# Seven block products for eight in the first feed-forward step's way down, with raw weights asked for two chunks ahead

## The chip, the cores and the metric

One core of one Trainium2 chip. The metric is the device time of one execution in microseconds (us). The engines are TensorE (PE: matmuls, PEld: its weight loads), VectorE (DVE), ScalarE (ACT), GpSimd (POOL) and SyncE (SP); SP and POOL also issue the transfers (DMA), each from a queue of its own that runs in order.

## The reference

One layer of a hybrid decoder over 576 rows (512 of a prompt, 8 x 8 of samples), 1024 channels wide, all in float32:

```python
x = x + 0.5 * swiglu(rmsnorm(x, ffn1_norm), w_gate, w_up, w_down)   # 2816 hidden channels
x = x + concat(y_lru, y_pool) @ w_out                               # mixer, from rmsnorm(x) @ w_in
x = x + cross_attend(rmsnorm(x, xattn_norm), mem_k, mem_v, wq, wo)  # 4 heads, 256 memory rows
x = x + 0.5 * swiglu(rmsnorm(x, ffn2_norm), w_gate, w_up, w_down)
y = rmsnorm(x, final_norm)

def swiglu(x, w_gate, w_up, w_down):
    return (silu(x @ w_gate) * (x @ w_up)) @ w_down
```

The change lies in the two feed-forward steps, called f1 and f2 here, which share one function.

## The kernel before, in words

Activations stand with channels on the 128 partitions and the 576 rows along the free side, so x is eight panels of 128 x 576. Each float32 operand is split into a high and a low part (`split`, L175 to L182: ACT rounds the high part, DVE subtracts it), and each product is three matmuls of high x high, high x low and low x high; a matmul has 128 x 128 weights and 288 columns, half of the rows.

**The way up.** The 2816 hidden channels are 22 chunks of 128. The first three of f1 and the first two of f2 are computed plainly (`std`). Every other chunk takes gate and up together as one 2 x 2 block product with seven block products for eight (Strassen's form, as Winograd wrote it), named by their weights: 11, E, F, G, 12, H and 22, twelve matmuls each. E, F, G and H are sums of the raw blocks 11, 12, 21 and 22. One pass of the loop over f (from L848) runs the products in the order 11, E, then 22 of the chunk before (`finish_chunk`), F, G, 12, H. `fill()` puts steps of the way down between them.

**The way down.** In f2, chunks 0 to 15 are taken in four groups of four (`quick`), again with seven products for eight: a column is a pair of output panels of one group, seven products of six matmuls in six steps, and there are 4 x 4 = 16 columns. Their weights come as `td` and `t2` tiles, split by `ensure`. The operands of such a group are sums of hidden chunks (`build_a`, `build_b`, into tiles `ph` and `pl`). The results go to SBUF on ACT (`take`, L659) and are added into x by an accumulating transfer on POOL's queue (L676, L703, L710). Chunks 16 to 21 go plainly (`down`, groups of two and four). In f1 all 22 chunks go plainly in five groups (`FGS`): each hidden chunk is split into `hh` and `hl`, 48 matmuls a chunk go into `pd`, and DVE adds the result into x (L554). The last group of each step runs alone after the loop; in f1 each panel of x is then squared and split for the mixer (`nm.add`).

**Where the block sums come from.** In f1 `prepare_a` and `prepare_b` load the four raw blocks (L440) and DVE makes four sums a chunk (L454 to L456, L467). In f2 two of them, for E and H, and two sums of the down weights, were made in memory earlier: `background` (L157) issues accumulating transfers on POOL's queue during f1 and the mixer into `gsum` and `dsum`. DVE makes the other two (L491, L492).

**What sets the order.** All matmuls of f1 and f2 keep their written order (`chain` in `mm`). The other engines' instructions, the transfers on SP among them, are put in order by a planner that takes what is ready by its own costs; on the chip each engine's queue then runs in that order and waits where something isn't there. Buffers limit how far ahead it goes: four tiles `wr` for raw weights (`WRB`, 4 KB a partition each), five each for the split parts `wh` and `wl` (`WSB`); one `td`. The same three tags hold all weight panels of the mixer and the attention, and there the caches too. At the start of f1 the two first panels and the squares of x by rows (`xs`, L756, five tiles in `wh` and `wl`, for the norm factor) use them.

Of the kernel before, what the change touches and what calls it, by code (L numbers as in the profile page):

```python
# [22 lines left out]
FGS = (4, 4, 4, 5, 5)  # L23
# [7 lines left out]
WRB, WSB = 4, 5  # L31
# [38 lines left out]
def hybrid_step(ctx, tc, a):  # L70
# [45 lines left out]
    neg = const.tile([P, 4 * DC], F32, name="neg")  # L116
    v.tensor_scalar(neg, cst[:, :4 * DC], -1.0, None, op0=ALU.mult)

    def ncol(name, i=0):
        c = _C[name] + i  # L120
        return neg[:, c:c + 1]


    s.activation(const.tile([P, 1], F32, name="table"), ones, AF.Silu)
# [22 lines left out]
    nfast = FFC - STD[1]  # L147
# [3 lines left out]
    for i in range(nfast):  # L151
        w = a["f2_gu"][i].rearrange("p b k n -> p b (k n)")
        jobs.append((gsum[i], w[:, 0:2, :], w[:, 3:4, :].to_broadcast([P, 2, KP * P])))
        if i < FAST * NQ:
            w = a["f2_d"][i // NQ, i % NQ].rearrange("p b k n -> p b (k n)")
            jobs.append((dsum[i // NQ][i % NQ], w[:, 0:2, :], w[:, 3:4, :].to_broadcast([P, 2, 2 * P])))
# [216 lines left out]
    def ffn(name, n, fp, turn, plain, head=False, fast=False):  # L373
# [3 lines left out]
        wstd, wgu, wd = a[f"{name}_s"], a[f"{name}_gu"], a[f"{name}_d" + "p" * fast]  # L377
# [7 lines left out]
        def small_tile(nm_):  # L385
            return fp.tile([P, HT], F32, tag="pc", bufs=2 if fast else 3, name=nm_)

        def full_tile(nm_):
            return fp.tile([P, T], F32, tag="e", bufs=3 if fast else 2, name=nm_)
# [30 lines left out]
        def std_out(i, pg, pu):  # L420
            e = full_tile("e")
            for (p, q), (_, rr) in zip(pieces(pg, e), pieces(pg, r)):
                v.tensor_mul(q, p, rr)
            s.activation(e, e, AF.Silu, scale=-1.0)
            v.tensor_mul(e, e, half)
            for p, q in pieces(pu, e):
                v.scalar_tensor_tensor(out=q, in0=p, scalar=-1.0, in1=q, op0=ALU.mult, op1=ALU.mult)
            if fast:
                raw[i] = e
            else:  # L430
                split(hh[0][:, i, :], hl[0][:, i, :], e)
# [3 lines left out]

        def load(f):
            if f < FFC:
                raws[f] = [raw_tile(f"r{i}") for i in range(2)]
                for i in range(2):
                    nc.sync.dma_start(raws[f][i], wgu[f - plain, :, 2 * i:2 * i + 2])  # L440
# [6 lines left out]
        def prepare_a(f):  # L447
            if f >= FFC:
                return
            r0, r1 = raws[f]  # L450
            (w22, w11), (w12, w21) = ([t[:, i] for i in range(2)] for t in (r0, r1))
            w = W[f] = {}
            w["22"], w["11"] = parts_of(r0, "a")
            v.tensor_add(w22, w22, w21)  # L454
            v.tensor_add(w21, w21, w11)
            v.tensor_add(w11, w11, w22)  # L456
            w["E"], w["F"] = parts_of(r0, "e")

        def prepare_b(f):
            if f >= FFC:  # L460
                return
            r0, r1 = raws.pop(f)
            w = W[f]
            one = [fp.tile([P, KP, P], F32R, tag=tag, name=f"{tag}_b") for tag in ("oh", "ol")]
            split(*one, r1[:, 0])
            w["12"] = lambda q, k: one[q][:, k, :]
            v.tensor_add(r1[:, 0], r1[:, 0], r0[:, 1])  # L467
            w["G"], w["H"] = parts_of(r1, "g")


        def load_pairs(f):
            if f < FFC:
                w, e = wgu[f - plain], gsum[f - plain].rearrange("p b (k n) -> p b k n", n=P)
                raws[f] = [raw_tile(f"r{i}") for i in range(2)]
                for (i, b), src in zip(((0, 0), (0, 1), (1, 0), (1, 1)), (e[:, 0], w[:, 1], w[:, 2], e[:, 1])):
                    nc.sync.dma_start(raws[f][i][:, b], src)

        def load_22(f):
            if f < FFC:
                raw22[f] = wp.tile([P, KP, P], F32, tag="wr", bufs=WRB, name="r22")  # L480
                nc.sync.dma_start(raw22[f], wgu[f - plain, :, 0])

        def prepare_e(f):
            if f < FFC:
                W[f] = {}
                W[f]["E"], W[f]["11"] = parts_of(raws[f][0], "e")

        def sum_g(f):
            if f < FFC:
                r0, r1 = raws[f]  # L490
                v.tensor_add(r0[:, 1], r0[:, 1], r0[:, 0])  # L491
                v.tensor_add(r0[:, 0], r0[:, 1], r1[:, 0])  # L492

        def prepare_g(f):
            if f < FFC:
                W[f]["G"], W[f]["F"] = parts_of(raws[f][0], "g")
# [12 lines left out]
        groups = PLAIN if fast else [(sum(FGS[:i]), FGS[i]) for i in range(len(FGS))]  # L509
        panels = [(gi, j) for gi in range(len(groups)) for j in range(DC)]  # L510
        fetched, wdown = {}, {}

        def fetch(i):

            if i < len(panels) and i not in fetched:
                gi, j = panels[i]
                c0, fg = groups[gi]
                c0 -= PLAIN[0][0] * fast
# [3 lines left out]
        def make(i, pool=None):  # L522

            if i < len(panels) and i not in wdown:
                fetch(i)
                gi, j = panels[i]
                if pool is None:
                    w = [fp.tile([P, groups[gi][1], P], F32R, tag=tag, bufs=2 + fast, name=f"{tag}{j}")
                         for tag in ("dh", "dl")]
                else:  # L530
                    w = [pool.tile([P, groups[gi][1], P], F32R, name=f"t{q}{j}") for q in "hl"]
# [3 lines left out]
        def down(gi, after=None):  # L535

            c0, fg = groups[gi]
            pd = {}

            def step(j, k):  # L540
# [8 lines left out]
                if k == fg - 1 and fast:  # L549
# [3 lines left out]
                elif k == fg - 1:  # L553
                    v.tensor_add(halves(x[:, j, :]), pd[j][:, :, :HT], halves(x[:, j, :]))  # L554
                    if after:
                        after(j)
# [9 lines left out]
        hh, hl = {}, {}  # L566

        def group(gi):
            for d, tag in ((hh, "hh"), (hl, "hl")):
                d[gi] = fp.tile([P, FGS[gi], T], F32R, tag=tag, bufs=2, name=f"{tag}{gi}")  # L570

        def hidden(f):

            if fast:
                b = 2 * (f % 2)
                return [q[:, b:b + 2, :].rearrange("p h n -> p (h n)") for q in pairs[f // 2]]
            gi = max(i for i in range(len(groups)) if groups[i][0] <= f)
            return [q[gi][:, f - groups[gi][0], :] for q in (hh, hl)]
# [36 lines left out]
        def fetch_main(i):  # L615

            if i < FAST * NQ:
                g, q = divmod(i, NQ)
                t = draw[i] = fp.tile([P, 4, 2, P], F32, tag="td", name=f"td{i}")
                nc.sync.dma_start(t[:, 0:4:3], dsum[g][q].rearrange("p b (k n) -> p b k n", n=P))  # L620
                nc.sync.dma_start(t[:, 1:3], a["f2_d"][g, q, :, 1:3])

        def fetch_22(i):
            if i < FAST * NQ:
                t = draw[i, 0] = fp.tile([P, 2, P], F32, tag="t2", name=f"t2{i}")
                nc.sync.dma_start(t, a["f2_d"][i // NQ, i % NQ, :, 0])

        def ensure(n):

            while made[0] < min(n, 4 * FAST * NQ):  # L630
# [3 lines left out]
                if k == 3:  # L634
                    split(*(q[:, 0] for q in w), draw.pop((i, 0)))
                    fetch_22(i + 1)
                else:
                    if k:
                        v.tensor_add(t[:, k], t[:, k], t[:, k - 1])
                    split(*w, t[:, k:k + 2])  # L640
                    if k == 2:
                        fetch_main(i + 1)
# [72 lines left out]
        if fast:  # L715
            ts = [fp.tile([P, 2, 3, HT], F32, tag=tag, bufs=3, name=f"t_{tag}") for tag in ("ph", "pl")]
        else:
            group(0)
            ts = [fp.tile([P, 2, 3, HT], F32, tag=tag, bufs=2, name=f"t_{tag}") for tag in ("hh", "hl")]
# [3 lines left out]
        if head:  # L723
# [7 lines left out]
            for k in range(DC):  # L731
                n.split(k)
                if k % 2 == 0:
                    for raw, hi, lo in ws:
                        split(hi[:, k:k + 2, :], lo[:, k:k + 2, :], raw[:, k:k + 2, :])
# [5 lines left out]
        w = panel(wstd[1, 0], DC, P, "s")  # L741
        std(cols(ps1[0]), w, range(4))
# [20 lines left out]
        else:  # L763
            q = row_factor([n.acc], n.name, free[2], parts=3)
            for i in range(2):
# [4 lines left out]
        std(cols(ps1[1]), w, range(4))  # L770
# [7 lines left out]
        if fast:  # L778
            half = r
        else:  # L780
            half = fp.tile([P, T], F32, name=f"half_{n.name}")
            s.activation(half, r, AF.Copy, scale=0.5)
        std(cols(ps1[1]), w, range(4, DC))
        std_out(0, *ps0)
        if fast:
            load_pairs(plain)
            load_22(plain)
            prepare_e(plain)
            sum_g(plain)
            std_out(1, *ps1)  # L790
            prepare_g(plain)
            load_pairs(plain + 1)
            fetch_main(0)
            fetch_22(0)
        else:
            load(plain)
        if fast:
            pass
        elif plain > 2:
            ps2 = accumulators(2)  # L800
            std(cols(ps2[0]), panel(wstd[2, 0], DC, P, "s"), range(DC))
            std_out(1, *ps1)
            if head:
                n.sums(3, ts[1][:, 1])
            std(cols(ps2[1]), panel(wstd[2, 1], DC, P, "s"), range(DC))
# [816 lines left out]
```

## Time and profile before

| what | us |
|---|---|
| median of 3 runs (lowest to highest) | 1138.15 (1137.78 to 1138.83) |
| the profiled execution: its time, its span | 1138.62, 1136.7 |
| f1, start to the mixer's first product | 0 to 401.9 |
| of it the loop's first product, the last group of the way down | 50.7, 367.6 |
| mixer and attention | 401.9 to 742 |
| f2: first product, last group of the way down | 742, 1097.8 |
| PE, DVE, ACT, POOL busy in the span | 1118.5, 832.0, 610.9, 134.4 |
| granted TensorE clock | 0.996 |

A group's line gives code line, engine, operation, output and inputs, shape and count, then busy time in us and the mean ns of one, then the engine's idle time before it and what ended it. Matmuls overlap, so the mean of one (295 ns) is longer than the distance between two. A line of the chain of waits is start, length and what ran; a line of waits is who waited, for whom, us in total, times, longest.

### The profile page before, as it was taken

The numbers are of one execution on the slowest core, as the hardware profiler recorded it, in microseconds if no ns is written. First come the engines' busy times: TensorE is split into PE (matmuls) and PEld (weight loads), VectorE is DVE, ScalarE is ACT, GpSimd is POOL, SyncE is SP. The second block draws the span as 40 slices with busy tenths as digits, with TensorE's granted clock in tenths as the row PEclk, the third lists the DMA queues.
The fourth block names the chain that finished last, engine by engine and source line by source line (L and its number), as shares of the span: only waits on it lengthen the run. The fifth ranks groups of instructions, "written<-read, shape, count | busy, mean of one in ns | idle before, by whom it ended". The sixth has DMA issues, their size and how long they took to land.

```text
span 1136.7 us, 21329 instructions
## 1 busy us (share of the span) xinstructions
PE 1118.5 (98%) x8536; PEld 1101.0 (97%) x8536; DVE 832.0 (73%) x1387; ACT 610.9 (54%) x1052; POOL 134.4 (12%) x176
## 2 busy tenths in 40 slices
PE   8999999999999999999999999999999999999996
PEld 8999999999999999999999889999999999999996
DVE  8877778777775687986833566769878888787654
ACT  7644344344342454885622455546666666666554
POOL 0011111111111033310000000000121111212110
PEclk9999999999999999999999999999999999999998
DMA  8356766577674388642566762223675766766652
GB/s 293 117 146 152 185 167 149 140 162 188 155 182 107 103 236 191 119 141 94 174 217 215 261 229 92 66 89 93 162 176 148 182 172 160 188 167 154 148 115 84
DMA packets 82547, 179.58 MB, mean 158 GB/s; under 512 B 8272, under 2 KB 28752, under 8 KB 82320
## 3 DMA queue, kind: packets, MB, share of 16 engines
q1 hardware_dynamic: 55456, 129.66, 35.3%
q0 software_dynamic: 24064, 45.88, 22.9%
q10 hardware_dynamic: 2928, 2.67, 0.7%
q8 instruction: 67, 1.10, 0.4%
q14 instruction: 32, 0.26, 0.1%
HBM read 156.86 MB, written 34.17 MB: 168 GB/s over the span
## 4 chain that ended last, share of the span: by engine, by line
PE 91%; DVE 4%; ACT 2%; DMA 2%; issue 1%; DVEq 0%; SPq 0%; ACTq 0%
PE pu L136 23%; PE pd L136 15%; PE pc L136 11%; PE d L136 7%; PE pa L136 5%; PE q L136 5%; PE wo L136 5%; PE xo L136 5%; PE pg L136 3%; PE k L136 2%; PE v L1347 2%; PE in_l L136 2%; PE in_p L136 2%; PE o L136 1%; PE s L136 1%
## 5 line engine op out<-in xcount | busy, mean ns | idle before, releaser
L136 PE MATMUL pd<-hh,dl 128*128 128x288 f32 x352 | 75.3, 295 | 0.0
L136 PE MATMUL pd<-hh,dh 128*128 128x288 f32 x352 | 75.0, 294 | 0.0
L136 PE MATMUL pd<-hl,dh 128*128 128x288 f32 x352 | 75.0, 294 | 0.0
L178 ACT CAST wh_e<-r 128x1024 fp32r<-128x1024 f32 x39 | 41.0, 1051 | 57.1 <-DVE r L456 27.5
L136 PE MATMUL d<-ph,dh 128*128 128x288 f32 x224 | 66.8, 298 | 0.2 <-ACT add_e L659 0.2
L136 PE MATMUL d<-ph,dl 128*128 128x288 f32 x224 | 66.3, 296 | 0.0
L136 PE MATMUL d<-pl,dh 128*128 128x288 f32 x224 | 66.0, 295 | 0.0
L676 POOL DMA_DIRECT2D x<-add_e x16 | 19.3, 1204 | 380.9 <-ACT dh L178 348.6
L136 PEld LDWEIGHTS pd<-hh,dh 128*128 128x128 f32 x352 | 56.3, 188 | 0.0
L136 PEld LDWEIGHTS pd<-hh,dl 128*128 128x128 f32 x352 | 56.2, 188 | 0.0
L136 PEld LDWEIGHTS pd<-hl,dh 128*128 128x128 f32 x352 | 56.1, 188 | 0.0
L179 DVE TENSOR_TENSOR wl_e<-r,wh_e 128x1024 fp32r<-128x1024 f32 x39 | 47.7, 1222 | 11.1 <-ACT wh_e L178 11.1
L178 ACT CAST wh_g<-r 128x1024 fp32r<-128x1024 f32 x39 | 41.0, 1052 | 20.2 <-DVE r L467 14.4
L179 DVE TENSOR_TENSOR wl_g<-r,wh_g 128x1024 fp32r<-128x1024 f32 x39 | 47.7, 1222 | 5.2 <-ACT wh_g L178 4.1
L178 ACT CAST dh<-wr_d 128x512 fp32r<-128x512 f32 (+2 forms) x50 | 30.9, 619 | 34.5 <-PE pd L136 14.7
L136 PE MATMUL pu<-n1l,wh_a 128*128 128x288 f32 x152 | 44.9, 295 | 0.0
L136 PE MATMUL pu<-n1h,wl_a 128*128 128x288 f32 x152 | 44.8, 295 | 0.0
L136 PE MATMUL pu<-n1h,wh_a 128*128 128x288 f32 x152 | 44.7, 294 | 0.0
L907 ACT ACTIVATE g<-g 128x576 f32<-128x576 f32 x39 | 26.8, 686 | 32.2 <-DVE g L906 32.2
L136 PEld LDWEIGHTS d<-ph,dh 128*128 128x128 f32 x224 | 42.1, 188 | 0.8 <-ACT add_e L659 0.4
L136 PEld LDWEIGHTS d<-pl,dh 128*128 128x128 f32 x224 | 42.3, 189 | 0.0
L179 DVE TENSOR_TENSOR dl<-td,dh 128x512 fp32r<-128x512 f32 x48 | 33.1, 689 | 12.5 <-ACT dh L178 9.3
(561 smaller groups left out, 4235.3 us busy)
## 6 DMA issues: line engine op xcount, KB each, us to landing
gsum<-f_gu POOLq DMA_DIRECT2D x40, 512.0 KB, 8.6
r<-f_gu SPq DMA_DIRECT2D x38, 512.0 KB, 4.1
r<-f_gu SPq DMA_DIRECT2D x60, 256.0 KB, 4.1
x<-add POOLq DMA_DIRECT2D x40, 288.0 KB, 4.4
r<-gsum SPq DMA_DIRECT2D x40, 256.0 KB, 3.9
dsum<-f_d POOLq DMA_DIRECT2D x32, 256.0 KB, 5.7
ck<-ck SPq DMA_DIRECT2D x16, 512.0 KB, 4.4
cv<-cv SPq DMA_DIRECT2D x16, 512.0 KB, 7.2
```

The source lines that it names most:

```text
L136: i = te.matmul(*args, **kw)
L178: s.copy(hi, src)
L179: v.tensor_tensor(out=lo, in0=src, in1=f(hi), op=ALU.subtract)
L676: nc.gpsimd.dma_start(x[:, j:j + 2, HT:], t, accum_op=ALU.add)
L907: s.activation(g, g, AF.Silu, scale=-1.0)
L1347: te.matmul(ps[:, m, :HD], lhsT=lhs[:, kd, ms], rhs=w[wi][:, k, :], start=kd == 0 and i == 0, stop=kd == DC - 1 and i == 2)
```

## The change

Of f1's way down, chunks 0 to 15 take the form that f2 has: `quick`, `build_a`, `build_b`, and the adds into x by transfers. The plain form of f1 goes with all its helpers (`FGS`, `group`, `hh`, `hl`, `load`, `prepare_a`, `prepare_b`, `half`); f1's last group has four chunks for five. `head` now marks f1 in the shared function: there the down weights come raw, and DVE makes two more sums a column.

In both steps the weights of the way up come raw, 11 and 21 in one tile, 12 in another, 22 in a third, all asked for two chunks ahead, for which `WRB` goes to 6 and `WSB` to 4. H = 21 + 11 and G = F + 12 are made on DVE; E = 21 + 22 and F = 11 + E are made by accumulating transfers on POOL's queue, the first from memory, the second within SBUF. So block 22 is read twice, and `gsum` with its forty transfers is gone. The sixteen jobs for f2's down weights now run beside the projections of the mixer and `w_out` alone. The inputs' blocks are stored in another order (21, 11, 12, 22).

```diff
-FGS = (4, 4, 4, 5, 5)
...
-WRB, WSB = 4, 5
+WRB, WSB = 6, 4
...
-    gsum = [scratch.tile([P, 2, KP * P], F32, name=f"gsum{i}") for i in range(nfast)]
...
-        jobs.append((gsum[i], w[:, 0:2, :], w[:, 3:4, :].to_broadcast([P, 2, KP * P])))
...
+        def load_11(f):
             if f < FFC:
+                raws[f] = [raw_tile("r0")]
+                nc.sync.dma_start(raws[f][0], wgu[f - plain, :, 0:2])
+
+        def load_12(f):
+            if f < FFC:
+                raws[f].append(raw_tile("r1"))
+                nc.sync.dma_start(raws[f][1][:, 0], wgu[f - plain, :, 2])
+
+        def sum_eh(f):
+            if f < FFC:
+                r0, r1 = raws[f]
+                v.tensor_add(r1[:, 1], r0[:, 0], r0[:, 1])
+                nc.gpsimd.dma_start(r0[:, 0], wgu[f - plain, :, 3], accum_op=ALU.add)
...
         def prepare_e(f):
             if f < FFC:
                 W[f] = {}
+                r0 = raws[f][0]
+                W[f]["E"], W[f]["11"] = parts_of(r0, "e")
+                nc.gpsimd.dma_start(r0[:, 1], r0[:, 0], accum_op=ALU.add)
+
+        def prepare_g(f):
             if f < FFC:
                 r0, r1 = raws[f]
-                v.tensor_add(r0[:, 1], r0[:, 1], r0[:, 0])
                 v.tensor_add(r0[:, 0], r0[:, 1], r1[:, 0])
+                W[f]["G"], W[f]["F"] = parts_of(r0, "g")
...
-                if k == fg - 1 and fast:
+                if k == fg - 1 and after:
+                    xj = halves(x[:, j, :])
+                    v.scalar_tensor_tensor(out=xj, in0=pd[j][:, :, :HT], scalar=0.5, in1=xj, op0=ALU.mult, op1=ALU.add)
+                    after(j)
...
+                if head:
+                    nc.sync.dma_start(t[:, 0:3], wq[g, q, :, 0:3])
+                else:
+                    nc.sync.dma_start(t[:, 0:4:3], dsum[g][q].rearrange("p b (k n) -> p b k n", n=P))
+                    nc.sync.dma_start(t[:, 1:3], wq[g, q, :, 1:3])
...
+                    elif head:
+                        v.tensor_add(t[:, 3], t[:, 0], t[:, 1])
+                        v.tensor_add(t[:, 0], t[:, 0], draw[i, 0])
...
         w = panel(wstd[1, 0], DC, P, "s")
+        load_11(plain)
+        load_12(plain)
...
+        mid = 6 if head else 4
+        std(cols(ps1[1]), w, range(mid))
```

In the loop over f the calls now stand so, between the products:

```python
product(U, w["11"], n, N11, True)      # first pass: load_11(f + 2)
product(C, w["E"], n, T1, True)        # then prepare_h(f), load_12(f + 2); first pass: sum_eh(f + 1)
finish_chunk(before)                   # then the pair operands, prepare_e(f + 1)
product(U, w["F"], n, T2, False)       # then prepare_22(f), load_22(f + 2)
product(C, w["G"], n, N22, False)      # then sum_eh(f + 2)
product(A, w["12"], n, N21, False)
product(U, w["H"], n, T3, False)       # then prepare_g(f + 1), load_11(f + 3)
```

At the start of f1 the first block sums (`sum_eh(plain)`) follow the first plain chunk, and the split for E and 11 the first half of the third; in both steps the loads for the second looped chunk and the first `td` follow ahead of the loop.

More of the change, by code (lines that the diff above doesn't have):

```diff
@@ L787, in ffn @@
             load_22(plain)
             prepare_e(plain)
-            sum_g(plain)
+            load_11(plain + 1)
+            load_12(plain + 1)
             std_out(1, *ps1)
[L791 to L805, printed above, removed]
-            prepare_a(plain)
-            std_out(2, *ps2)
-        else:
-            prepare_a(plain)
-            std_out(1, *ps1)
@@ L811, in ffn @@
[L811 to L828 removed]
+        load_22(plain + 1)
+        fetch_pair(0)
```

272 lines of the change are left out of this document (91 added, 181 removed).

## The prediction

> **What bounds the kernel now.** I read the page's totals first, then TensorE's waits, then stretches of each step, then one chunk of the second step in order of time.
>
> ```profile
> span 1136.7 us, 21329 instructions
> PE 1118.5 (98%) x8536; PEld 1101.0 (97%) x8536; DVE 832.0 (73%) x1387; ACT 610.9 (54%) x1052; POOL 134.4 (12%) x176
> PE 91%; DVE 4%; ACT 2%; DMA 2%; issue 1%; DVEq 0%; SPq 0%; ACTq 0%
> ```
>
> TensorE is busy for all but 18.2 us and carries 91% of the chain that ended last. Its waits, longest first:
>
> ```profile
> PE pg L136 <- ACT wh L178: 5.5, 1, 5.5
> PE rs L136 <- DVE rf_f L272: 1.9, 2, 1.4
> PE pg L136 <- DVE rf_n L272: 1.3, 1, 1.3
> ...
> PE d L136 <- ACT add_e L659: 0.2, 1, 0.2
> PE pd L136 <- DVE pl L179: 0.2, 1, 0.2
> ```
>
> The start (5.5), the norm factor of the first step (1.3) and the tail are the only waits of size; inside the two loops nothing over 0.2 us is left. Stretches of the first step's loop and way down, and of the second step's beginning and middle (columns: PE, PEld, DVE, ACT, POOL busy; clock; DMA share; GB/s):
>
> ```profile
> 300.00:340.00 40.00, 40.00 (x305) 40.00 (x304) 29.93 (x45) 16.38 (x25) 6.38 (x8) 1.00 0.73 179
> 367.00:402.00 35.00, 35.00 (x265) 35.00 (x264) 23.59 (x31) 17.28 (x25) 0.00 (x1) 1.00 0.41 123
> ...
> 770.00:820.00 50.00, 50.00 (x380) 50.00 (x379) 44.89 (x78) 31.94 (x60) 4.22 (x4) 1.00 0.50 129
> ...
> 860.00:900.00 40.00, 40.00 (x303) 39.87 (x302) 34.20 (x59) 27.34 (x56) 6.17 (x7) 1.00 0.66 163
> ...
> 980.00:1020.00 40.00, 40.00 (x303) 39.91 (x302) 31.85 (x55) 26.94 (x54) 7.17 (x7) 1.00 0.66 164
> ```
>
> PE is full in each, at clock 1.00. So a matmul taken away shortens the kernel by its own spacing, as long as the others keep pace. The second step already runs the seven-product way down, and its stretches show that DVE (32 to 34 of 40 us) and ACT (27) keep pace there.
>
> **The change, part by part.** First the products. The first step's way down today, the second step's, and a run of matmuls without a gap:
>
> ```profile
> L136 PE MATMUL pd<-hh,dl 128*128 128x288 f32 x352 | 75.3, 295 | 0.0
> L136 PE MATMUL pd<-hh,dh 128*128 128x288 f32 x352 | 75.0, 294 | 0.0
> L136 PE MATMUL pd<-hl,dh 128*128 128x288 f32 x352 | 75.0, 294 | 0.0
> ...
> L136 PE MATMUL d<-ph,dh 128*128 128x288 f32 x224 | 66.8, 298 | 0.2 <-ACT add_e L659 0.2
> ```
> ```profile
> 367.56 34.38 PE pd L136 x258
> ```
>
> Before: 3 x 352 = 1056 matmuls for 22 chunks, so 48 a chunk. After: 16 chunks by blocks, as the second step does, 3 x 224 = 672; six chunks plainly, 6 x 48 = 288; together 960. Removed are 96. They overlap (295 ns each), so the price is the spacing, 34.38 / 258 = 0.133 us: **96 x 0.133 = -12.8 us**. All of them stood in stretches with PE full. The rest of the step's matmuls is unchanged.
>
> Next the work beside them. In the first step DVE loses two of four weight sums a chunk, its split of each hidden chunk and most adds into x; it gains operand sums, more down splits, and two sums of `td` a column that the second step had from memory. Rather than net these I take the second step's loop, which is the same code, and add the `td` sums. The loop's period there:
>
> ```profile
> 875.00 1.59 PE pc L136 x12
> ...
> 893.27 1.59 PE pc L136 x12
> ...
> 900.50 1.58 PE pc L136 x12
> ...
> 910.83 1.59 PE pc L136 x12
> ...
> 915.60 1.59 PE pu L136 x12
> ```
> ```profile
> L639 DVE TENSOR_TENSOR td<-td 128x256 f32<-128x256 f32 x32 | 13.4, 420 | 0.3
> L491 DVE TENSOR_TENSOR r<-r 128x512 f32<-128x512 f32 x20 | 13.7, 687 | 0.1
> ```
>
> A chunk takes 910.83 - 893.27 = 17.6 us (product E to product E). By the stretches DVE has 31.85/40 to 34.20/40 of it to do, 14.0 to 15.0 us; about 3.1 us stay free. A column is six steps and a chunk runs seven, so the first step adds 7/6 x 2 x 0.42 = 1.0 us and keeps about 2.1. DVE stays behind TensorE's cover: 0. In the second step the sums for H and G are two of L491's size, as today, so DVE is unchanged there. ACT's 27 of 40 covers the new copies.
>
> The sums E and F become accumulating transfers on POOL's queue, 2 x 39. The trace has no such transfer that anyone soon waits for. The nearest are the adds into x:
>
> ```profile
> x<-add POOLq DMA_DIRECT2D x40, 288.0 KB, 4.4
> x<-add_e POOLq DMA_DIRECT2D x16, 288.0 KB, 6.4
> ```
> ```profile
> L178 ACT CAST wh_e<-r 128x1024 fp32r<-128x1024 f32 x39 | 41.0, 1051 | 57.1 <-DVE r L456 27.5
> ```
> ```profile
> 890.64 1.22 DVE L179 TENSOR_TENSOR wl_e<-r,wh_e 128x1024 fp32r<-128x1024 f32 x1
> 898.25 1.23 DVE L179 TENSOR_TENSOR wl_g<-r,wh_g 128x1024 fp32r<-128x1024 f32 x1
> ```
>
> E of the next chunk is asked for a chunk ahead, so its 4.4 to 6.4 us hide. F is the tight one: split of E, transfer, G's sum, split, product F. With four weight buffers for five, the split of the next E can start only when this chunk's E product ends, 893.27 + 1.59 = 894.9 (today it ended at 891.9). ACT and DVE then need 1.05 + 1.22 = 2.3 us: 897.2. The transfer lands at 901.6 to 903.6, G's sum of 0.69 ends at 904.3 at the latest, its split (2.3) at 906.6; G's buffer is free from 900.50 + 1.58. Product F of the next chunk starts at 915.60, so **about 9 us are left**. I take 0.5 us over both loops; the ends are 0 and a stall in every chunk (the third rival). A page of the Trainium skill, "DMA: Bandwidth & Descriptors", section on the SWDGE path, fits a POOL-issued transfer as 2.0 us plus bytes over 436 GB/s; for 256 KB that estimate is 2.6 us, where the rows above say 4.4 and 6.4. By the page F would have some 11 us left, and the sum would be 0.5 us lower; the measurement decides.
>
> The queues. POOL's runs in order, and the transfers for F stand among the adds into x, which wait for ACT; behind F's transfer waits G's sum, and behind that all of DVE. SP's loads come two chunks ahead and wait for one of six buffers; `td` stands behind them:
>
> ```profile
> 813.75 7.74 DMA td<-f_d
> ```
> ```profile
> POOL x L676 <- ACT add_e L659: 32.3, 8, 4.3
> SPq L476 <- DVE wl L179: 72.4, 9, 13.8
> DVE r L454 <- DMA r<-f_gu: 11.8, 7, 4.1
> ```
>
> SP already stands up to 13.8 us before such a load, and DVE waited seven times for raw weights (11.8 us) in the first step, with PE full; asking earlier can win only that hidden wait. 0.
>
> The **head**. The norm factor ends the 1.3 us wait:
>
> ```profile
> 21.25 7.79 DMA xs<-xs
> ```
> ```profile
> 29.06 1.06 ACT L757 ACTIVATE xs<-xs 64x1024 f32<-64x1024 f32 x1 [0.17 <-DMA xs<-xs]
> ```
> ```profile
> 33.09 1.16 PE L136 MATMUL pg<-ident,rf_n 128*128 128x128 f32 x8 [1.33 <-DVE rf_n L272]
> ```
>
> Today only the last of five `xs` tiles waits for the first panels' buffers; with four buffers three do. If they land together, two more squares stand in the chain, 2 x 1.06 = +2.1 us or a little more. Against it, two more k-steps (12 matmuls, 1.6 us) now run before the factor is wanted, and the raw weights no longer queue in between. Ends: -1.3 (the wait is gone) and +0.8; I take 0.
>
> The first chunk now has the pair operands of two pairs and the last norm sums at once, with no way-down steps to pass the time. The second step's start is like it: DVE 44.89 of 50, and PE full. Between 0 and +4 (two pairs at some 2 us more than the chunk can hold); I take +0.5, near that row. At the end of the step eight panels of 24 matmuls (3.2 us each) face x's add, split, square sum and panel split of four chunks on DVE: 23.59 us over eight panels is 2.9 us today. It just fits; the last hidden chunk's split has 18 matmuls to hide behind for 24, and where the second step has that it cost 0.2 (`pl`): +0.2. The mixer and attention get four split buffers for five and six raw ones for four; 0, between -0.5 and +0.5, since three panels of 6.4 us (48 x 0.133) still stand ahead. The block sums in memory for the second step's way down (POOL) move from the loop to the projections, where such jobs ran already: 0.
>
> The profiled execution took 1138.6 us with a span of 1136.7. 1138.6 - 12.8 + 0.5 + 0.5 + 0.2 = **1127.0**; it lay 0.5 above the median of the runs, 1138.15, so the forecast is **1126.5 us**. Its own range is 1123.5 to 1129.
>
> **Rivals.** (1) *Part is given back*, 1129 to 1135: the first chunks' DVE queue (+4), or `td` stuck behind waiting raw loads on SP. For: DVE 90% busy at 770 to 820, SP's 13.8. Against: no wait of PE over 0.2 there. At the middle of it, +5: 1131.5.
> (2) *The head gains too*: the 1.3 us go and no stall comes: 1138.15 - 12.8 - 1.3 = 1124.0, and with a half more in the middle 1123.5.
> (3) *Slower: G's sum on DVE waits for F's transfer.* DVE runs in order; if each chunk's sum is reached w us before the transfer lands, DVE loses w, has 2.1 us free in the first step and 3.1 in the second, and the rest falls on PE. From 19 x (w - 2.1) = 11.6, w = 2.7 us, the gain is gone; at w = 3.1 it costs 19 us: 1145.5. For: 4.4 against 6.4 us of landing is 2.0 us of spread, and a blocked add into x holds POOL up to 4.3. Against: 9 us of slack, in which DVE has other work ready.
> (4) *It doesn't do what it says*: the loads come no earlier, because buffers free no earlier. Then the products still go: 1126.5. Only if `td`, whose landing after 7.74 us stands in today's chain, came later by 0.8 us in each of the 16 columns would 12.8 be lost and the time stay at 1138.
>
> **How the numbers follow.** Forecast 0.58, with (4)'s first form in it; part given back 0.22; head gains 0.06; slower 0.09; no change 0.05. This measurement tells 0.2% from nothing, so faster is below 1135.9 and slower above 1140.4: faster 0.86, same 0.05, slower 0.09. 1123 to 1134 takes in the forecast, the head's gain and most of (1).
>
> **What would show it.** The first step's way down with 672 matmuls on `d` and 288 on `pd`; the mixer's first product near 389 us, for 401.9; PE with 40 of 40 us in the first step's loop; no DVE wait over 2 us on a POOL transfer; a PE wait at the norm factor between 0 and 2 us. I am wrong if DVE waits for `r` by transfer about 3 us a chunk, or PE waits on `wh_g`, `dh` or `add_e` in the loops.

## The result, and the profile after

The kernel became slower: 1245.63 us (1245.16 to 1248.56) against 1137.97 us (1135.68 to 1138.83) for the kernel before on the same chip, four runs each. The ratio is **1.0955** (95% interval 1.0932 to 1.0978). The forecast was 1126.5 us with a range up to 1134.

The page of the changed kernel begins with the span and the engines; the third line is its chain of waits by engine:

```profile
span 1243.8 us, 21744 instructions
PE 1142.7 (92%) x8440; PEld 1111.9 (89%) x8440; DVE 842.0 (68%) x1478; ACT 674.0 (54%) x1251; POOL 223.6 (18%) x270
...
PE 11%; DMA 9%; issue 5%; DVE 4%; ACT 2%; POOL 2%; DVEq 0%; POOLq 0%; ACTq 0%; SPq 0%
```

The 96 matmuls are gone (8536 to 8440). But TensorE now stands for 1243.8 - 1142.7 = 101.1 us, where it stood 18.2 us. The chain could be followed back only to 831.9 us, so its shares add up to 33%; TensorE has 11 of these 33, where it had 91 of 100 before. Its busy time rose by 24.2 us although 12.8 us of matmuls are missing, so 37 us of it are not explained by the number of matmuls. The granted clock fell from 0.996 to 0.977; an estimate from that is 1243.8 x 0.019 = 24 us. The other 13 us weren't told apart.

The waits of the changed kernel (who waited, for whom, us in total, times, longest):

```profile
DVE r L464 <- DMA r<-r: 125.1, 34, 7.2
ACT wh_g L172 <- DVE r L464: 108.9, 33, 6.2
...
PE d L135 <- ACT add L619: 28.1, 17, 2.6
PE d L135 <- ACT d L642: 25.8, 11, 4.5
PE d L135 <- ACT add_e L619: 21.9, 8, 4.5
...
PE pg L135 <- DVE rf_n L266: 0.4, 1, 0.4
```

L464 is G's sum on DVE, and `r<-r` is F's accumulating transfer within SBUF. DVE waited for it 34 times in 39 chunks, 3.7 us a time. ACT waited for DVE with G's split for 108.9 us, and in the three lines of the way down that are shown TensorE waited for ACT for 75.8 us. Before, all waits of TensorE in the loops were 0.2 us or less. The last line is the wait at the norm factor, 1.3 us before.

Stretches of the changed kernel, one of f1's loop and two of f2's (columns as before: PE, PEld, DVE, ACT, POOL busy; clock; DMA share; GB/s):

```profile
300.00:340.00 40.00, 35.39 (x258) 33.98 (x256) 28.10 (x50) 21.42 (x43) 8.28 (x9) 1.00 0.63 138
860.00:900.00 40.00, 34.83 (x258) 33.95 (x257) 26.72 (x48) 22.09 (x47) 9.46 (x10) 1.00 0.73 157
920.00:960.00 40.00, 34.27 (x228) 33.80 (x228) 26.90 (x47) 20.50 (x43) 9.43 (x10) 0.88 0.71 156
```

Where TensorE was busy for 40 of 40 us, it is for 34 to 35, in both loops alike. DVE, ACT and POOL each do less in a stretch than they could, so none of them is the bound by its amount of work. In the last stretch the same busy time holds only 228 matmuls, at clock 0.88.

One chunk of f2 shows how it hangs together. DVE in order of time (start, length, what; in brackets the wait before it):

```profile
904.97 1.23 DVE L173 TENSOR_TENSOR wl_e<-r,wh_e 128x1024 fp32r<-128x1024 f32 x1 [0.66 <-ACT wh_e L172]
906.17 0.42 DVE L173 TENSOR_TENSOR dl<-t,dh 128x256 fp32r<-128x256 f32 x1
906.62 0.46 DVE L771 TENSOR_TENSOR g<-pu,g 128x288 f32<-128x288 f32 x1
907.14 0.69 DVE L173 TENSOR_TENSOR wl<-r,wh 128x512 fp32r<-128x512 f32 x1
915.00 0.69 DVE L464 TENSOR_TENSOR r<-r,r 128x512 f32<-128x512 f32 x1 [7.16 <-DMA r<-r]
915.61 0.68 DVE L173 TENSOR_TENSOR dl<-td,dh 128x512 fp32r<-128x512 f32 x1
```

POOL in the same stretch:

```profile
907.27 1.19 POOL L636 DMA_DIRECT2D x<-add_e  x1 [3.45 <-ACT wh L172]
908.77 0.92 POOL L459 DMA_DIRECT2D r<-r  x1 [0.31 <-issue]
```

ACT, and TensorE behind it:

```profile
915.77 1.04 ACT L172 CAST wh_g<-r 128x1024 fp32r<-128x1024 f32 x1 [3.42 <-DVE r L464]
916.72 0.40 ACT L619 ACTIVATE add<-d 128x288 f32<-128x288 f32 x1
```
```profile
917.18 0.40 PE L135 MATMUL d<-ph,dh 128*128 128x288 f32 x1 [2.64 <-ACT add L619]
```

The split of E ends at 906.2. In DVE's order G's sum stands only three short instructions behind it, so DVE comes to it at 907.8. F's transfer can be issued from 906.2 on, but on POOL an add into x stands first and holds the queue until 908.46. The transfer is issued at 908.77 and lands at 914.9. DVE stands for 7.16 us, with ready work behind the sum. ACT's next instruction is the split of G, so ACT stands too. Behind it stands `add<-d`, the copy that takes a finished result of the way down out of the bank that TensorE wants next. So TensorE stops for a sum whose product is far off: product F, the first to use that split, starts at 925.96.

### The profile page after: what moved, and what is told of

It is laid out like the page before. It is cut to its first block, busy times and chain, and to the rows that moved or that the text cites. A ratio compares the mean times of both kernels' runs of the same rounds, so it can differ in the third digit from the quotient of the medians.

```text
span 1243.8 us, 21744 instructions
## 1 busy us (share of the span) xinstructions
PE 1142.7 (92%) x8440; PEld 1111.9 (89%) x8440; DVE 842.0 (68%) x1478; ACT 674.0 (54%) x1251; POOL 223.6 (18%) x270
## 5 line engine op out<-in xcount | busy, mean ns | idle before, releaser
L135 PE MATMUL d<-ph,dh 128*128 128x288 f32 x448 | 140.7, 314 | 79.8 <-ACT add L619 28.1
L135 PEld LDWEIGHTS d<-ph,dh 128*128 128x128 f32 x448 | 86.5, 193 | 91.2 <-ACT add L619 32.1
L135 PE MATMUL d<-pl,dh 128*128 128x288 f32 x448 | 134.9, 301 | 0.0
L135 PE MATMUL d<-ph,dl 128*128 128x288 f32 x448 | 134.6, 300 | 0.0
L464 DVE TENSOR_TENSOR r<-r,r 128x512 f32<-128x512 f32 x39 | 27.0, 692 | 137.5 <-DMA r<-r 125.1
L172 ACT CAST wh_g<-r 128x1024 fp32r<-128x1024 f32 x39 | 40.9, 1048 | 127.3 <-DVE r L464 108.9
L135 PEld LDWEIGHTS d<-ph,dl 128*128 128x128 f32 x448 | 87.0, 194 | 0.0
L135 PEld LDWEIGHTS d<-pl,dh 128*128 128x128 f32 x448 | 86.9, 194 | 0.0
L172 ACT CAST dh<-td 128x512 fp32r<-128x512 f32 x96 | 59.4, 618 | 32.4 <-DVE td L596 16.4
L619 ACT ACTIVATE add<-d 128x288 f32<-128x288 f32 x128 | 52.2, 408 | 5.4 <-PE d L135 4.5
L173 DVE TENSOR_TENSOR wl_h<-r,wh_h 128x1024 fp32r<-128x1024 f32 x39 | 47.5, 1217 | 3.1 <-ACT wh_h L172 3.1
L172 ACT CAST wh_e<-r 128x1024 fp32r<-128x1024 f32 x39 | 41.0, 1050 | 13.2 <-PE pc L135 12.5
L172 ACT CAST wh_h<-r 128x1024 fp32r<-128x1024 f32 x39 | 40.8, 1046 | 11.8 <-PE pu L135 9.3
```

The source lines that it names most:

```text
L135: i = te.matmul(*args, **kw)
L172: s.copy(hi, src)
L173: v.tensor_tensor(out=lo, in0=src, in1=f(hi), op=ALU.subtract)
L619: s.activation(dst, src, AF.Copy, scale=0.5 * sign)
```

## The experiments

All kernels are made from the changed one. "Theory A" in the expectations is: DVE runs in order and stands at G's sum for F's transfer. The table has every kernel; f1, the middle and f2 are split by the first products of the mixer and of f2 in the profiled execution.

| kernel | time, us | f1 | middle | f2 |
|---|---|---|---|---|
| before | 1137.97 | 401.8 | 340.1 | 394.8 |
| changed | 1245.63 | 445.2 | 341.5 | 457.1 |
| F by DVE | 1149.24 | 405.9 | 341.5 | 400.8 |
| E by DVE, F by transfer | 1216.75 | 426.3 | 341.5 | 447.1 |
| E and F by DVE | 1156.19 | 405.4 | 341.5 | 408.1 |
| G's sum late | 1192.19 | 416.7 | 341.6 | 426.9 |
| G's sum late, `td` once | 1137.09 | 396.5 | 341.6 | 397.2 |
| `td` once alone | 1218.87 | 430.5 | 341.6 | 445.0 |
| F by DVE, `td` once | 1137.31 | 394.9 | 341.6 | 399.0 |
| the same, without `td`'s head sums | 1136.31 | 395.4 | 341.6 | 397.6 |
| F by DVE, two `td`, five raw tiles | 1142.98 | 403.3 | 341.6 | 396.1 |
| the same, F by an instruction of POOL | 1155.47 | 409.8 | 341.5 | 400.7 |
| F by DVE, four raw and five split tiles | 1209.89 | 437.8 | 340.3 | 429.6 |
| G's sum late, two `td`, five raw tiles | 1195.64 | 438.1 | 341.5 | 412.7 |

### F made by DVE

```diff
-                nc.gpsimd.dma_start(r0[:, 1], r0[:, 0], accum_op=ALU.add)
...
+                v.tensor_add(r0[:, 1], r0[:, 1], r0[:, 0])
                 v.tensor_add(r0[:, 0], r0[:, 1], r1[:, 0])
```

> Change kept, but F = 11 + E is made by DVE ahead of G's sum instead of by a transfer within SBUF (39 transfers fewer on POOL, 39 sums of 0.69 us more on DVE). Theory A (DVE stands in its queue at G's sum until F's transfer has landed, 125 us in 34 waits): the waits go, f1 ends near 390 us and the time is 1126 to 1136, about 1130. Rival B (POOL's queue is the cause: E's transfers and the adds into x hold each other up): at most half comes back, about 1195. Rival C (the seven-product way down overloads DVE in f1 whatever makes the sums): f2 recovers its 60 us, f1 still ends near 445 us, time about 1185.

Measured: 1149.24 us (1147.70 to 1150.13), ratio to before 1.0097 (1.008 to 1.0114). 39 sums of 0.69 us more on DVE made the kernel 96 us faster than the changed one. Theory A's mechanism holds; rivals B and C, which stood at about 1195 and 1185, fall as the main cause. But A's own number, 1126 to 1136, was too good: 13 us or more stayed lost. TensorE's longest wait in the loops and a wait of DVE in this kernel:

```profile
PE d L135 <- ACT add_e L619: 7.6, 9, 1.2
```
```profile
DVE td L598 <- DMA td<-f_d: 19.6, 12, 3.1
```

The waits at G's sum are gone, and DVE's longest wait for a transfer is now for `td`, the way down's weights.

### E made by DVE, F by transfer; then both by DVE

```diff
-                nc.gpsimd.dma_start(r0[:, 0], wgu[f - plain, :, 3], accum_op=ALU.add)
+                v.tensor_add(r0[:, 0], r0[:, 0], raw22[f])
```

> Change kept, but E = 21 + 22 is made by DVE from the raw block 22 that is loaded anyway; F stays a transfer within SBUF. Theory A: F's transfer is the one that is waited for, so the time stays near 1240 (1225 to 1255), with DVE waiting some 3 us a chunk for it. Rival B (POOL's queue): with 39 POOL transfers gone and none between the adds into x and F's transfer, most comes back, 1150 or less. Rival C: about 1245.

> Both E and F made by DVE, no weight sum by transfer in either step; the seven-product way down, the loads two chunks ahead and the buffer counts kept. It shows the products alone. Theory A: 1127 to 1140 (DVE has four sums a chunk, 16.8 of 17.6 us in f1, so a few us may come on top). Rival B: the same. Rival C: f1 still ends near 445 us, 1185 or more.

Measured: 1216.75 us with F's transfer kept (one run), and 1156.19 us (1153.56 to 1158.97; ratio 1.0163, 1.0143 to 1.0182) with both by DVE. With E by DVE most of the wait at G's sum stays:

```profile
DVE r L464 <- DMA r<-r: 97.7, 36, 6.6
```

(In both kernels block 22 of the first looped chunk is also loaded earlier, since E's sum now reads it.) Both times lie outside what theory A expected, 1225 to 1255 and 1127 to 1140. So it is F's transfer that is waited for: taking it away gains 96 us. Taking E's away gains 29 us, and the wait for F's falls by 27 us with it. That part fits rival B (E's transfers on POOL's queue make F's later), though DVE's order changed with it. Where F's is gone, taking E's away too loses 7 us, but that isn't the price of the sums alone: DVE then stands at E's sum for the raw block 22, 31.1 us in 34 waits. E's own reader is not held up: in the changed kernel's list of waits ACT doesn't stand at E's split for a transfer. E's transfer is asked for a chunk ahead and has the time it needs, as the prediction had it.

### G's sum held back

All transfers stay. G's sum is tied to the last instruction of product H of the chunk before, which moves it back in DVE's order.

```diff
-                v.tensor_add(r0[:, 0], r0[:, 1], r1[:, 0])
+                i = v.tensor_add(r0[:, 0], r0[:, 1], r1[:, 0])
+                if f > plain:
+                    tc.add_manual_dep(i.ins, latest[0].name, ...)
```

> Change kept with all its transfers; only G's sum is bound to come after product H of the chunk before, so that it stands some 15 places behind the split of E in DVE's queue instead of 7. Nothing is taken off POOL or DVE. Theory A: the transfer then lands while DVE has other work, the wait for it falls from 3.2 us a chunk to under 0.5, time 1127 to 1140. Rival B: no change, about 1245, since POOL's queue is as before. Rival C: no change in f1, about 1185 to 1245.

Measured: 1192.19 us (1186.91 to 1195.19), ratio 1.0474 (1.0444 to 1.0504), 53 us better than the changed kernel with the same work and the same transfers, though theory A had expected 1127 to 1140. The wait at G's sum, 125.1 us before, is nearly gone, and others have come up:

```profile
DVE dl L173 <- ACT dh L172: 49.2, 28, 4.5
...
DVE td L601 <- DMA td<-f_d: 28.2, 14, 4.2
...
DVE r L464 <- DMA r<-r: 1.5, 2, 1.0
```
```profile
PE d L135 <- ACT add L622: 29.0, 26, 2.3
```

One refill of `td` in this kernel, DVE's last split of the old column and SP's loads of the next:

```profile
909.42 0.69 DVE L173 TENSOR_TENSOR dl<-td,dh 128x512 fp32r<-128x512 f32 x1
```
```profile
910.14 0.53 SPq L584 DMA_DIRECT2D td<-dsum  x1
910.72 0.66 SPq L585 DMA_DIRECT2D td<-f_d  x1
```

The load goes out 0.03 us after the split ends. SP was not late here: there is one `td` tile, it is free only when its last reader is done, and what is loaded is wanted at once. The next split of it on DVE starts at 919.0. It is the same at all 30 refills of this kernel, 15 in each step: the load (in f2 the first of two) goes out at most 0.08 us after the last split.

### `td` loaded once

The two kernels above again, with `td` loaded for the first column of each step and used for all sixteen. So 30 columns' loads are left out, and these kernels don't compute the reference's result.

```diff
-                t = draw[i] = fp.tile([P, 4, 2, P], F32, tag="td", ...)
+                if not i:
+                    t = draw[i] = fp.tile([P, 4, 2, P], F32, tag="td", ...)
...
+                if i:
+                    t = draw[i] = draw[0]
+                elif head:
                     nc.sync.dma_start(t[:, 0:3], wq[g, q, :, 0:3])
```

> F made by DVE, `td` loaded for the first column alone and used again by the other 15 (their loads are left out, all sums and splits stay). Theory A2: all of the `td` wait goes, 1125 to 1132. Rival D (DVE's work): 1143 or more.

> G's sum late as in the run before, all weight sums by transfer kept; the `td` tile is loaded for the first column alone and used again by the other 15 (their loads are left out, all sums and splits stay). Theory A2 (with G's sum late, SP stands longer at the raw load behind it and `td` comes late): 1130 to 1145 for 1192. If F's transfer still costs by itself (POOL's queue, rival B): 1175 or more.

> The changed kernel, with F's transfer as it is, but in both steps the tile td is loaded for the first of the 16 columns alone and used for all (30 td loads are left out, so the down weights of the other columns are not the reference's; the small t2 is still loaded). Theory A, DVE stands at G's sum for F's transfer: that wait stays, L464 near 125 us, and the time with it: 1205 to 1245 us. Theory T, the late td tile is the main cause and F's wait only its shadow: 1140 to 1160, with L464's wait under 30 us.

Measured, one run each: 1137.31 us with F by DVE (11.9 less than with the loads), 1137.09 with G's sum late (55.1 less), and 1218.87 where nothing else is altered (26.8 less). The last two lie where theory A2 and theory A had them; the first is 5 us above A2's 1125 to 1132. In the kernel with nothing else altered the wait at G's sum is as it was:

```profile
DVE r L464 <- DMA r<-r: 124.1, 37, 6.9
```

So `td` alone is not the cause, and theory T falls. With G's sum late and `td` out of the way, the 39 transfers for F cost next to nothing against 39 sums on DVE, and win nothing either (1137.09 and 1137.31). A distance that is enough for a sum is seen there; DVE in order of time in the kernel with the late sum and `td` once:

```profile
874.30 1.23 DVE L173 TENSOR_TENSOR wl_e<-r,wh_e 128x1024 fp32r<-128x1024 f32 x1 [0.65 <-ACT wh_e L172]
...
886.66 0.68 DVE L464 TENSOR_TENSOR r<-r,r 128x512 f32<-128x512 f32 x1
```

The sum stands 11.1 us behind the end of E's split (875.5) and waits for nothing. In the changed kernel's chunk DVE came to it after 1.6 us.

### Two `td` tiles

A second `td` tile, for which one raw tile is given up.

```diff
-WRB, WSB = 6, 4
+WRB, WSB = 5, 4
...
-                t = draw[i] = fp.tile([P, 4, 2, P], F32, tag="td", ...)
+                t = draw[i] = fp.tile([P, 4, 2, P], F32, tag="td", bufs=2, ...)
```

> F made by DVE, and two `td` tiles for one, paid for by five raw weight buffers for six. Theory A2 (what is left after F, 23 us over the forecast, is DVE standing at the sums of `td` until its load has landed, since the single tile is asked for only when the column before has been read): f1 ends near 392 us for 405.9, time 1127 to 1136. Rival D (DVE's own work, 88% of f1's loop, is too much): no better than 1149, f1 still ends past 402. Rival E (raw loads two chunks ahead are needed): slower than 1149.

> The changed kernel whole, all its transfers kept, with G's sum held back until product H of the chunk before (1192.2 with one td tile) and two td tiles, for which the raw tiles go from six to five. If the two causes found, DVE standing at G's sum and the single td tile refilled 5 us after its last reader, are all of the loss of size, DVE is spared the 27 us of sums that the kernel with F by DVE and two td tiles (1143.0) has, and the time is 1137 to 1143; below 1137 it would beat the kernel before. If instead the five raw tiles hold the loads for the transfers back (four of them cost 61 us), or the late sum makes the split of G late for its product, it is 1150 to 1190, with waits of DVE or ACT on a transfer from f_gu into r of over 1 us a chunk.

Measured with F by DVE: 1142.98 us (1140.47 to 1145.48), ratio 1.0042 (1.0029 to 1.0056). That is 6.3 less than with one `td` tile and the best time of a changed kernel that does the whole computation; it doesn't reach the kernel before. Theory A2 had expected 1127 to 1136 and an end of f1 near 392 us; f1 ends at 403.3, and DVE still waits 9.4 us for `td`. Rival D, no better than 1149, and rival E, slower than that, fall by the time, though f1 does end past 402 us, as D had it.

Measured with G's sum late and both transfers: 1195.64 us (1191.59 to 1197.23), ratio 1.0499 (1.0469 to 1.0529). This was expected at 1137 to 1143 and is no better than with one `td` and six raw tiles (1192.19). Lines of this kernel's waits, one load of `td` on SP, and DVE around it:

```profile
SPq L452 <- DMA r<-r: 108.7, 26, 8.6
```
```profile
DVE td L601 <- DMA td<-f_d: 28.2, 13, 5.5
...
ACT wh_e L172 <- DMA r<-f_gu: 19.7, 4, 6.0
```
```profile
159.45 0.92 SPq L582 DMA_DIRECT2D td<-f_d  x1
```
```profile
158.74 0.68 DVE L173 TENSOR_TENSOR dl<-td,dh 128x512 fp32r<-128x512 f32 x1
...
168.19 0.43 DVE L601 TENSOR_TENSOR td<-td 128x256 f32<-128x256 f32 x1 [4.99 <-DMA td<-f_d]
168.53 0.45 DVE L829 TENSOR_TENSOR g<-g,rstd_n 128x288 f32<-128x288 f32 x1
```

The wait for `td` is as large as with one tile (28.2 us in 13 waits, for 28.2 in 14). SP isn't late here either: the load goes out 0.03 us after the split that reads the tile last ends, at 159.42. But with two tiles DVE's first sum of a column stands a whole column earlier in its order, ahead of all three splits of the column in between, and again DVE stands at it until the load has landed, 4.99 us here, with work of the way up (L829) behind it. As with G's sum, the planner put the reader early, and the second tile bought nothing.

The five raw tiles cost as well. The raw tile that F's transfer writes is held until that has landed and the late sum and split are done. SP stands at raw loads for it for 126.6 us in all (108.7 of them in the line shown), where it stood 94.6 us with six tiles and one `td`; ACT now stands at E's split for 19.7 us, which it didn't with six, and DVE at H's sum for 24.5 us, for 21.9. That is over 1 us a chunk, the sign that the expectation named for this rival, at a time somewhat above its 1150 to 1190. How the loss divides between `td` and the raw tiles wasn't told apart.

### The rest of the loss

First the two sums of `td` at the head of each column of f1 (here block H is loaded raw and the sums are left out), in the kernel with F by DVE and `td` once:

```diff
-                    elif head:
-                        v.tensor_add(t[:, 3], t[:, 0], t[:, 1])
-                        v.tensor_add(t[:, 0], t[:, 0], draw[i, 0])
```

> The kernel with F by DVE and td loaded once (1137.3), from which in f1 the two head sums of td are left out as well (32 instructions of DVE, 13.4 us by the rows of before; f1's down weights are then not the reference's). Theory D, the rest of the loss in f1 is DVE's work: f1 ends 2 to 5 us sooner (394.9 now), 1132 to 1135. Theory S, the rest is the four split buffers: f1 ends within 1 us of 394.9, 1136 to 1138.

Measured: 1136.31 us, one run, 1.0 less; f1 took 395.4 us for 394.9. 13 us of DVE's work in f1 are worth nothing there, and theory D falls. A line of TensorE's waits in the kernel with F by DVE and `td` once shows where 4.6 us of the rest go:

```profile
PE d L135 <- ACT add_e L622: 4.6, 6, 0.8
```

There are three in each step, 68 us apart, which is once in four chunks: the way down wants a bank whose result ACT has not yet copied out. In the kernel before, this wait was 0.2 us, once.

Then the buffers of before:

```diff
-WRB, WSB = 6, 4
+WRB, WSB = 4, 5
```

> The kernel with F by DVE (1149.2), with the buffers as before the change: four raw tiles and five split tiles for six and four. Theory S, four split buffers cost the rest: 1142 to 1147, ACT's waits on PE for wh gone. Theory R, SP stands longer before a raw load when four tiles are there, td behind it comes later, and with it the split for the way down: 1150 to 1165, and DVE's waits for td longer than 19.6 us.

Measured: 1209.89 us (1208.45 to 1212.71), ratio 1.0639 (1.0621 to 1.0657), 61 us worse than with six and four. Theory S falls as it was put. R's direction holds, but not its size (1150 to 1165) nor its sign, since DVE's waits for `td` are not longer than 19.6 us; the waits are at the raw blocks themselves:

```profile
DVE r L446 <- DMA r<-f_gu: 27.4, 20, 4.5
...
DVE td L598 <- DMA td<-f_d: 15.8, 7, 3.6
```
```profile
ACT wh_e L172 <- DMA r<-f_gu: 31.2, 12, 4.0
```

H's sum waits for raw loads and E's split for the transfer that adds block 22. So four raw tiles are too few for this form of the way up. The middle took 340.3 us in this kernel and 341.5 or 341.6 in all others of the change, so the four split tiles (or having more than four raw ones) cost the middle 1.2 to 1.3 us.

### F on the engine POOL

```diff
-                v.tensor_add(r0[:, 1], r0[:, 1], r0[:, 0])
+                nc.gpsimd.tensor_add(r0[:, 1], r0[:, 1], r0[:, 0])
```

> The kernel with F made by DVE and two td tiles (1143.0) but F now made by an instruction of the engine POOL, for 39 sums of 0.69 us on DVE; no transfer lands. No row shows such a sum on POOL; between 0.69 us (DVE's) and 3 us. If the length of the transfer (5.9) and not POOL's place in the order was the trouble, there is no wait of DVE over 1 us a chunk at L464, and by theory D (DVE too full in f1, 27 us less in all) the time falls to 1132 to 1139; by theory S (four split buffers set the rest) it stays at 1140 to 1144. If POOL's order is the trouble (its adds into x hold it up to 13 us), DVE waits for POOL and it is 1150 to 1200.

Measured: 1155.47 us (1153.88 to 1156.45), ratio 1.0161 (1.0144 to 1.0178), 12.5 worse than with the same sum on DVE. The group of the sums on POOL, and in the same kernel the group of DVE's splits of 22 (its `wl<-r,wh`):

```profile
L463 POOL TENSOR_TENSOR r<-r 128x512 f32<-128x512 f32 x39 | 66.8, 1712 | 122.4 <-DVE wl_e L173 122.4
```
```profile
L173 DVE TENSOR_TENSOR wl<-r,wh 128x512 fp32r<-128x512 f32 x39 | 56.9, 1459 | 5.0 <-ACT wh L172 4.6
```

And the same splits in the kernel with F by DVE and two `td` tiles (shortest, median, longest in ns):

```profile
L173 DVE TENSOR_TENSOR wl<-r,wh x39: 678/683/693, 56.7 to 1085.6; 128x512 fp32r<-128x512 f32 x39
```

DVE waited for POOL's sum only 5.0 us in all, so the waiting by which the expectation got to 1150 to 1200 wasn't the trouble. But the split of 22 takes 1.46 us on the mean for 0.68. So 39 x 0.78 = 30 us go on DVE for the 27 us of sums that it was spared. One pair of them shows where; POOL, then DVE:

```profile
823.85 1.66 POOL L463 TENSOR_TENSOR r<-r 128x512 f32<-128x512 f32 x1
```
```profile
824.14 1.93 DVE L173 TENSOR_TENSOR wl<-r,wh 128x512 fp32r<-128x512 f32 x1
```

DVE's split begins within POOL's sum and ends 0.56 us after it. These 3 us net are not the 12.5; how the rest of it comes about wasn't told apart.

## Why the prediction was wrong

**The step that failed** is the one that priced F's transfer: "Product F of the next chunk starts at 915.60, so about 9 us are left. I take 0.5 us over both loops". The 9 us are the room of TensorE: they lie between the end of G's split and the product. But the first that wants the landing is not the product. It is G's sum, and where that stands in DVE's order is set by the planner's costs, not by when its product is due. It stood 1.6 us behind E's split in the chunk shown, where the transfer, behind an add into x, needed 8.7 us (906.2 to 914.9). Its landing (median 5.9 us) lay within the 4.4 to 6.4 that were assumed; the size of the transfer wasn't wrong, the place of its reader was. So a term of 0.5 us stood where 96 us came back with F's transfer taken away. The sign that the prediction had named for being wrong, DVE waiting for `r` by transfer about 3 us a chunk, came: 125.1 / 39 = 3.2 us. The page's DMA part lists it so (bytes each, median us from issue to landing):

```profile
r<-r POOLq DMA_DIRECT2D x39, 256.0 KB, 5.9
```

The fit of the Trainium skill's page "DMA: Bandwidth & Descriptors", section on the SWDGE path, gave an estimate of 2.6 us for this transfer; the row's 5.9 us decides. (The "some 11 us" that the prediction left to F by it come out at 12.8 when its own sum is redone, 915.6 - 902.8; it rests on the same room of TensorE and changes nothing.)

**The slower rival named the mechanism and missed the price.** It had DVE lose w us a chunk and TensorE only what exceeds DVE's free time of 2.1 and 3.1 us. With the measured w of 125.1 / 39 = 3.2 us its formula gives 19 x (3.2 - 2.1) + 20 x (3.2 - 3.1) = 23 us, so about 1150. The loss over the forecast was 119 us. Free time on DVE doesn't help: ACT stands at G's split right behind (108.9 us), and behind it the copies that free TensorE's banks, so in the chunk shown the wait reaches TensorE at once, whatever DVE could still catch up. In the rival's "Against", DVE "has other work ready"; it had, but behind the sum, and an engine in order can't reach it. Nor was the fall of the clock in the formula.

**Part given back** came as well, as a second cause, but not by the way named. "`td` stuck behind waiting raw loads on SP" was priced at +5. Doing away with `td`'s loads gained 11.9 us with F by DVE, 26.8 with nothing else altered, and 55.1 with G's sum late. But in all 30 refills of the changed kernel, too, SP issues the load within 0.1 us of the last split of the tile. The time from there to the landing is what DVE stands for, since the tile's next reader comes soon in its order. Leaving the loads out also takes them off SP's queue and the DMA engines; the runs don't part the two.

**The products** were right. 96 matmuls went, and the starts of two matmuls in an unbroken run lie 0.13 us apart in the traces of both kernels. In f1 the three kernels without `td`'s late loads end it at 394.9 to 396.5 us for 401.8, so 5 to 7 of the 12.8 us show there. f1 was to end near 389.

**The head** was taken at 0 with ends of -1.3 and +0.8. TensorE's wait at the norm factor went from 1.3 to 0.4 us, but that wasn't gained: the loop's first product starts at 51.9 us in the changed kernel's profiled execution, for 50.7 before, with the same 322 matmuls ahead of it. In six other kernels with six raw tiles it starts at 49.8 to 51.8 us. What the three `xs` tiles that wait cost in that isn't shown.

**The middle** was taken at 0, within 0.5; it cost 1.4 us (340.1 to 341.5), 1.2 to 1.3 of which go with the buffers of before.

**First chunks** (+0.5) and the **end of f1** (+0.2) drown in the waits of the loop and weren't measured apart.

**What stays open.** With both causes out of the way the kernel takes 1137 us, not 1126.5. 1.5 us of the 11 are the middle; the rest is 6 to 8 us in f1 against 389 and 2 to 4 in f2 (397.2 and 399.0 for 394.8). DVE's two sums a column are not it. Where F is made by DVE, 4.6 us of it are TensorE's six waits for ACT's copy `add_e`; with F's transfer and the late sum they are 0.3 us and the time is the same, with other small waits in their place. The runs don't say whether the number of split tiles has a part, since the one run with five of them took two raw tiles away as well.

## What to carry to other kernels

Moving a sum from a busy engine to a transfer can pay only if the reader of the result stands far enough behind in its own engine's order (and here it gained nothing even then, 1137.09 for 1137.31): look at when that engine reaches the reader, not at when the product is due. Where the order is made by a planner, count the distance between the instruction that releases the transfer and its reader, and give the transfer its queue's delay on top of its landing (here 8.7 us in all, for 5.9). A wait on an in-order engine is handed on to every engine that waits for something behind it, so the wait isn't paid out of slack on the waiting engine. A buffer that a transfer writes is held longer, which delays the loads behind it in the queue. And a second buffer helps only if the planner doesn't move the reader forward with it.

## What the runs showed of the hardware

**The clock falls around TensorE's waits.** TensorE's first matmul after a wait in f2 of the changed kernel, and the two stretches of 5 us from there:

```profile
936.24 0.61 PE L135 MATMUL d<-ph,dh 128*128 128x288 f32 x1 [3.75 <-ACT add_e L619]
```
```profile
935.00:940.00 5.00, 3.76 (x15) 3.76 (x16) 3.26 (x6) 2.46 (x6) 1.20 (x1) 0.52 0.37 78
940.00:945.00 5.00, 5.00 (x32) 5.00 (x32) 3.68 (x6) 2.63 (x5) 0.00 (x0) 0.79 0.65 150
```

After 3.75 us without a matmul the granted clock is 0.52 in the first stretch and 0.79 in the next, and 15 matmuls take the 3.76 us that would hold 28 at 0.133 us each. The wait is paid a second time in slower matmuls. The length of the wait alone doesn't settle it. Two other waits of the same kernel, with the stretch behind each:

```profile
875.51 0.40 PE L135 MATMUL d<-ph,dh 128*128 128x288 f32 x1 [3.12 <-ACT d L642]
958.58 0.40 PE L135 MATMUL d<-ph,dh 128*128 128x288 f32 x1 [1.99 <-ACT d L642]
```
```profile
875.00:880.00 5.00, 4.49 (x34) 4.49 (x35) 4.20 (x8) 3.21 (x7) 0.00 (x0) 1.00 0.43 131
959.10:962.50 3.40, 3.40 (x17) 3.40 (x16) 2.21 (x4) 1.49 (x3) 0.00 (x0) 0.50 0.50 153
```

After 3.12 us the clock stays at 1.00, after 1.99 us it falls to 0.50. The Trainium skill's page "TensorE: Matmul & The Clock Gate", Part 1, says that the clock is halved after an idle window of about 3.4 us and comes back after as long a busy one. The halving agrees, and so does the wait of 3.75 us; the one of 1.99 us is shorter than the page's window, and there the rows decide.

**A sum on POOL slows DVE.** DVE's split of 0.68 us took 1.46 us on the mean in the kernel in which POOL makes F's sums; in the pair shown it ran beside such a sum and its end followed POOL's by 0.56 us. The Trainium skill's page "SBUF — State Buffer", section "Who interferes with whom", says that a DVE instruction with two inputs in SBUF and a GpSimd instruction that reads SBUF can't run together and that the later one is blocked; the pair agrees.
